# Two transformer blocks on one core: stacked query parts, state-space weights on ScalarE, 512-column token-major products

## The chip, the cores and the metric

The kernel runs on one core of a Trainium2 chip. The metric is the device time of one execution in microseconds (us). The engines are TensorE (PE; its weight loads are listed apart as PEld), VectorE (DVE), ScalarE (ACT), GpSimd (POOL) and SyncE (SP), which issues the transfers.

## The reference

Two blocks act one after the other on 512 tokens of 1024 features, in 32-bit floating point. What the change touches lies nearly all in the first:

```python
proj = h @ w_in                       # q, k, v, z, xbc, dt, two gates
attn = windowed_gqa_sink(q, k, v, attn_sink)      # 16 heads of 64, 4 key heads
ssd = ssd_branch(z, xbc, dt_raw, ...)             # 32 heads of 64 in 8 groups
merged = sigmoid(gate_a) * (attn @ w_attn_branch) + sigmoid(gate_b) * (ssd @ w_ssd_branch)
x = x + merged @ w_out
x = x + cross_attention(rmsnorm(x), rmsnorm(mem), w_xq, w_xkv, w_xo)
x = x + square(relu(rmsnorm(x) @ w_up)) @ w_down
```

In the attention a block of 128 queries sees 384 keys (256 at the ends), with a linear bias by distance and a sink. The state-space part works on chunks of 128 tokens, forward and backward, with step sizes `dt` of their own. Inside a chunk, token `l` takes from token `s` the product of C and B, times the decay `exp(cs[l] - cs[s])`, times the step of `s`: the forward direction for `l >= s`, the backward one for `l <= s`, both on the diagonal. Chunk states carry the rest, and a skip `d_skip * x` is added. The second block (gated delta rule, sparse attention, a mixture of experts) ends its mixing with `x + merged @ w_out_2`.

## The kernel before

Every dense product is made in split form: an operand is held as a rounded high part and the remainder, and `mm3` (L275) issues three matmuls, high by high (L277), high by low (L278) and low by high (L279). Weights come in units of 512 KB; `load_w` (L261) takes one into the buffer `wr`, ScalarE casts the high part `wh` (L269), VectorE, or for some units GpSimd, subtracts to get the low part `wl` (L272). There are two buffers each of `wh` and `wl`, so the cast of a unit waits until TensorE is done with the unit two before it.

`proj_b` (L281) makes feature-major products: 128 weight columns stand in the array and 512 tokens stream. `proj_a` (L303) and `add_units` (L866) make token-major ones: a tile of 128 tokens stands in the array and 256 weight columns stream; VectorE adds each result to the residual rows (L876). These are `w_out`, `w_xo`, `w_down` and, in the second block, `w_out2`.

In `attention`, the queries of two heads are one unit, `atH` high and `atL` low, one head in partitions 0 to 63 and the other in 64 to 127; the scores `sc` of a block of 128 queries are three matmuls with 64 rows. VectorE adds the bias and takes the maximum (L508).

The state-space part runs over eight groups of four heads. `ssd_in` projects and convolves (first tap on ScalarE, L631; the others on VectorE, L638). `ssd_p1` works chunk by chunk: GpSimd makes `xw` (L710) and the step matrix `D` (two masked multiplications L696, a sum L698), TensorE the chunk's states `st` (L717), evicted by ScalarE to `pv` (L721, L723). Rows of `cs` are read back from DRAM, spread over the partitions. Per head ScalarE subtracts the column value (L731) and VectorE subtracts that of the other direction and takes the smaller (L732). Then come the exponential on ScalarE (L734), two multiplications on VectorE (by `CB`, L735; by `D`, L736), the skip `sk` on GpSimd (L738), and the product `yd` (L741) of four 64-column matmuls. `ssd_p2` carries the states on (L759), makes `yo`, adds it head by head (L772), and multiplies by the gate; `ssd_p3` norms, transposes and splits into `yh`, `yl`.

A scheduler sets each engine's order when the program is built: it interleaves the inner part of a group with the dense products of others (`mm`), and an engine then works strictly in that order. A block of the program below is thus not a stretch of time.

Of the kernel before, what the change touches and what calls it, by code (L numbers as in the profile page):

```python
# [14 lines left out]
OP = mybir.AluOpType  # L15
# [23 lines left out]
def host_arrays(inp):  # L39
# [30 lines left out]
    out["w_out"] = units_a(f("w_out")[0])  # L70
# [3 lines left out]
    out["w_xo"] = units_a(f("w_xo")[0])  # L74
    out["w_up"] = units_bt(f("w_up")[0])
    out["w_down"] = units_a(f("w_down")[0])
# [26 lines left out]
    out["w_out2"] = units_a(f("w_out_2")[0])  # L103
# [42 lines left out]
    c[1] = i[:, None] <= i[None, :]  # L146
    c[2] = i[:, None] >= i[None, :]
# [20 lines left out]
class Emit:  # L168
# [30 lines left out]
    def psum(self, stack, n, mm, sa, sm):  # L199
        """the eight banks: dense products, two kinds of chains"""  # L200
# [30 lines left out]
    # ---------------------------------------------------------------- tools  # L231
# [71 lines left out]
    def proj_a(self, banks, units, act):  # L303
        """token-major: banks: psum tiles, two token tiles of 256 columns each; act(k, t) -> (hi, lo)"""
# [11 lines left out]
    def split(self, hi, lo, src, scale=None):  # L316
        """hi + lo = src * scale (scale: per-partition AP or None)"""
# [11 lines left out]
    def rstd(self, out, ss, n, eps=EPS):  # L329
        """out = (ss / n + eps) ** -0.5"""  # L330
# [5 lines left out]
    def rsqrt(self, v, eps, scale=1.0, tile=None):  # L336
        """(scale * v + eps) ** -0.5: a first guess from the bits, then Newton's iteration"""
# [13 lines left out]
    def norm_out(self):  # L351
        """where normed rows go, transposed and split: put(t, h, x) takes half a tile; hT(k) -> (hi, lo)"""
# [14 lines left out]
    def norm_T(self, gname):  # L367
        """rmsnorm of token-major tiles, transposed and split: step(t, x) takes a tile"""
# [16 lines left out]
    def consts(self):  # L385
# [3 lines left out]
        self.ident, self.MU, self.ML = c[:, 0:128], c[:, 128:256], c[:, 256:384]  # L389
# [59 lines left out]
    def attn_in(self):  # L449
        nc, a = self.nc, self.a  # L450
        # keys: natural and half-swapped, split
        kn = self.A("kn", (128, 2, 2, 512), F32)
        for m in range(2):
            ps = self.PM()
            self.proj_b(ps, [self.w0 if m == 0 else self.wb(8 + m)], self.hB, True)
            nc.scalar.copy(kn[:, 0, m, :], ps)
            nc.sync.dma_start(kn[0:64, 1, m, :], kn[64:128, 0, m, :])
            nc.sync.dma_start(kn[64:128, 1, m, :], kn[0:64, 0, m, :])
        self.kh = self.A("kh", (128, 2, 2, 512))
        self.kl = self.A("kl", (128, 2, 2, 512))  # L460
        for s in range(2):
            for m in range(2):
                self.split(self.kh[:, s, m, :], self.kl[:, s, m, :], kn[:, s, m, :])
# [7 lines left out]
    def attention(self):  # L471
        nc, a = self.nc, self.a
        # the result of a tile of queries takes the place of the queries
        self.atH = [self.A("atH") for _ in range(2)]
        self.atL = [self.A("atL") for _ in range(2)]
        for i in range(8):
            ps = self.PM()
            self.proj_b(ps, [self.wb(i)], self.hB)
            qh, ql = self.atH[i // 4][:, i % 4, :], self.atL[i // 4][:, i % 4, :]
            nc.scalar.activation(qh, ps, AF.Copy, scale=0.125)  # L480
            nc.vector.scalar_tensor_tensor(ql, ps, 0.125, qh.bitcast(F32), op0=OP.mult, op1=OP.subtract)
        for i in range(8):
            qh, ql = self.atH[i // 4][:, i % 4, :], self.atL[i // 4][:, i % 4, :]
# [4 lines left out]
            for hf in range(2):  # L488
# [3 lines left out]
                pr = slice(64 * hf, 64 * hf + 64)  # L492
                sw = 0 if hf == n % 2 else 1
                kh, kl = self.kh[pr, sw, n // 2, :], self.kl[pr, sw, n // 2, :]
# [5 lines left out]
                for b in range(4):  # L500
# [5 lines left out]
                    self.mm3(sc[:, :L], qh[pr, qs], ql[pr, qs], kh[:, k0:k1], kl[:, k0:k1], True, True)  # L506
# [44 lines left out]
    def dt_section(self):  # L551
# [45 lines left out]
        self.ncs = self.cp.tile([128, 4, 32], F32, name="ncs")  # L597
        nc.vector.tensor_scalar(self.ncs, self.cs[:, :, 0, :], -1.0, None, op0=OP.mult)
# [3 lines left out]
    def gates1(self, f0, f1):  # L602
        """tanh of the halved gates, feature-major, to DRAM"""
# [10 lines left out]
    def branch_a(self):  # L614
        """(1 + tanh(ga / 2)) * (attn @ Wa), feature-major, to DRAM"""
# [11 lines left out]
    def conv(self, ps, ct, ntap, first, silu_scale=True):  # L627
        """half of the centred depthwise convolution of a psum tile, then 2 * half * sigmoid = silu"""
# [15 lines left out]
    def ssd_in(self, g):  # L644
        """projections of group g: B, C, x (feature-major, convolved) and the doubled silu of z (token-major)"""
# [18 lines left out]
    def ssd_p1(self, g, inp):  # L664
        """the part inside the chunks, and the chunks' states"""
# [4 lines left out]
        # token-major x and B  # L670
# [20 lines left out]
        D = []  # L691

        def steps(c):
            d = [self.G("D", (128, 4, 128)) for _ in range(2)]
            for i, m in enumerate((self.MU, self.ML)):
                nc.gpsimd.tensor_tensor(d[i], m[:, None, :].to_broadcast([128, 4, 128]),  # L696
# [169 lines left out]
    def add_units(self, xs, src, nk, act, scale=1.0, last=True, then=None):  # L866
# [11 lines left out]
        if not last:  # L878
            return
# [1432 lines left out]
```

## Time and profile before

| | |
|---|---|
| median of 3 runs | 2178.56 us (2176.49, 2178.56, 2189.05) |
| profiled execution | span 2182.1 us; the page gives no other time for it |
| PE | 2033.9 us busy, 93% of the span, 11818 matmuls; mean granted clock 0.961 of full speed |
| DVE | 1362.7 us, 62% |
| ACT | 892.3 us, 41% |
| POOL | 504.9 us, 23% |
| moved | 266.71 MB, mean 122 GB/s |

The shares are averages over stages that differ. By the lines that run in them, attention lies at about 80 to 280 us of the span, the state-space part at 280 to 882, cross attention at 882 to 1040 with the output product of the mixing ahead of it, the feed-forward part at 1040 to 1360, and the second block behind it. A line of the trace gives the start, the busy time of the instruction (neighbours overlap, so the distance of two starts tells what one costs in a run of them), engine, line, operation, the names of output and inputs, the shape, and in brackets the idle time of the engine before it and what ended it.

### The profile page before, as it was taken

The page shows a single profiled execution, that of the slowest core. Times are in us where ns is not written, and L with a number is a line of the kernel's source. Part 1 is how long each engine was busy: PE and PEld are TensorE (multiplying, and loading weights), DVE is VectorE, ACT ScalarE, POOL GpSimd, SP SyncE. Part 2 cuts the span into 40 slices and gives each one's busy share as a digit, 9 for nine tenths or more (in the row PEclk, how much of TensorE's full clock was granted, in tenths as well). Part 3 has the DMA queues.
Part 4 walks back from the last instruction along what each step waited for, and adds up shares of the span by engine and source line. Part 5 has one row for each costly group of instructions (what it writes and reads, how often), then busy time and mean ns, then how long its engine had stood idle before and what let it go on. Part 6 is the DMA issues. An engine that isn't in the chain of part 4 may idle for free. (4 is left out here: it accounts for less than half of the span.)

```text
span 2182.1 us, 31237 instructions
## 1 busy us (share of the span) xinstructions
PE 2033.9 (93%) x11818; PEld 1730.2 (79%) x11818; DVE 1362.7 (62%) x2622; ACT 892.3 (41%) x1630; POOL 504.9 (23%) x515
## 2 busy tenths in 40 slices
PE   7999988989999988999999999899899999998995
PEld 7788877877787777888999999787878768886774
DVE  4566446786978765466334444667789452538885
ACT  4344434444545343254323222542232333246773
POOL 0000034034433142101111101503511110224444
PEclk9999999999999999999999999998899899998997
DMA  4211234323333254422222223224212104677976
GB/s 168 84 67 63 78 101 159 116 72 112 94 107 100 88 157 157 156 88 69 97 97 96 88 97 116 97 79 122 91 50 76 45 21 158 223 296 245 324 269 165
DMA packets 131302, 266.71 MB, mean 122 GB/s; under 512 B 22256, under 2 KB 67696, under 8 KB 127050
## 3 DMA queue, kind: packets, MB, share of 16 engines
q1 hardware_dynamic: 127690, 256.26, 35.5%
q0 software_dynamic: 3456, 8.39, 1.7%
q8 instruction: 95, 1.56, 0.3%
q14 instruction: 61, 0.50, 0.1%
HBM read 242.93 MB, written 25.35 MB: 123 GB/s over the span
## 5 line engine op out<-in xcount | busy, mean ns | idle before, releaser
L272 DVE TENSOR_TENSOR wl<-wr,wh 128x1024 fp32r<-128x1024 f32 (+1 forms) x272 | 316.4, 1164 | 288.9 <-ACT wh L269 277.9
L269 ACT CAST wh<-wr 128x1024 fp32r<-128x1024 f32 (+1 forms) x272 | 264.5, 973 | 548.5 <-PE mm L278 282.8
L279 PE MATMUL mm<-hTh,wl 128*128 128x512 f32 (+1 forms) x1056 | 412.4, 391 | 1.3 <-DVE wl L272 1.3
L277 PE MATMUL mm<-hTh,wh 128*128 128x512 f32 (+1 forms) x1056 | 411.9, 390 | 1.6 <-ACT hTh L320 0.9
L278 PE MATMUL mm<-hTl,wh 128*128 128x512 f32 (+1 forms) x1056 | 410.7, 389 | 0.8 <-DVE hTl L321 0.8
L279 PEld LDWEIGHTS mm<-hTh,wl 128*128 128x128 f32 x1056 | 203.4, 193 | 42.4 <-issue 5.1
L277 PEld LDWEIGHTS mm<-hTh,wh 128*128 128x128 f32 x1056 | 203.2, 193 | 39.6 <-issue 2.6
L278 PEld LDWEIGHTS mm<-hTl,wh 128*128 128x128 f32 x1056 | 203.2, 192 | 39.2 <-issue 3.2
L710 POOL TENSOR_TENSOR xw<-xt,dtT 128x256 f32<-128x256 f32 (+1 forms) x32 | 29.8, 932 | 551.4 <-ACT xt L678 551.4
L278 PE MATMUL mm<-wl,hTh 128*128 128x256 f32 x512 | 150.1, 293 | 0.0
L277 PE MATMUL mm<-wh,hTh 128*128 128x256 f32 x512 | 149.8, 293 | 0.0
L279 PE MATMUL mm<-wh,hTl 128*128 128x256 f32 x512 | 149.3, 292 | 0.0
L278 PE MATMUL mm<-wl,uh 128*128 128x256 f32 x512 | 145.0, 283 | 0.0
L279 PE MATMUL mm<-wh,ul 128*128 128x256 f32 x512 | 144.8, 283 | 0.0
L277 PE MATMUL mm<-wh,uh 128*128 128x256 f32 x512 | 144.7, 283 | 0.0
L876 DVE SCALAR_TENSOR_TENSOR x<-mm,x 128x256 f32<-128x256 f32 x152 | 57.5, 420 | 93.4 <-PE mm L279 92.8
L1042 POOL TENSOR_TENSOR ul<-r,uh 128x512 fp32r<-128x512 f32 x32 | 41.7, 1303 | 274.8 <-ACT uh L1041 274.8
L278 PEld LDWEIGHTS mm<-wl,hTh 128*128 128x128 f32 x512 | 100.9, 197 | 1.7 <-issue 0.7
L277 PEld LDWEIGHTS mm<-wh,hTh 128*128 128x128 f32 x512 | 100.8, 197 | 1.0 <-issue 0.2
L279 PEld LDWEIGHTS mm<-wh,hTl 128*128 128x128 f32 x512 | 100.8, 197 | 0.7 <-issue 0.5
L278 PEld LDWEIGHTS mm<-wl,uh 128*128 128x128 f32 x512 | 98.2, 192 | 0.5 <-DVE wl L272 0.2
L277 PEld LDWEIGHTS mm<-wh,uh 128*128 128x128 f32 x512 | 98.2, 192 | 0.3
(571 smaller groups left out, 4706.2 us busy)
## 6 DMA issues: line engine op xcount, KB each, us to landing
mr<-in_w_egu_dram SPq DMA_DIRECT2D x32, 1024.0 KB, 8.4
wr<-in_win_b_dram SPq DMA_DIRECT2D x59, 512.0 KB, 3.3
cs<-csd SPq DMA_DIRECT2D x64, 256.0 KB, 4.5
wr<-in_w_up_dram SPq DMA_DIRECT2D x32, 512.0 KB, 3.3
wr<-in_w_down_dram SPq DMA_DIRECT2D x32, 512.0 KB, 3.3
wr<-in_w_ed_dram SPq DMA_DIRECT2D x32, 512.0 KB, 4.5
wr<-in_w_b_dram SPq DMA_DIRECT2D x29, 512.0 KB, 3.3
wr<-in_win_a_dram SPq DMA_DIRECT2D x18, 512.0 KB, 3.3
```

What stands on the lines that cost most here:

```text
L269: nc.scalar.copy(w.hi, raw)
L272: e.tensor_tensor(w.lo, raw, w.hi.bitcast(F32), op=OP.subtract)
L277: mm(out, lh, rh, start=start, stop=False, skip_group_check=skip)
L278: mm(out, lh, rl, start=False, stop=False, skip_group_check=skip)
L279: mm(out, ll, rh, start=False, stop=stop, skip_group_check=skip)
L710: nc.gpsimd.tensor_tensor(xw[:, d0:d1], h3(xt[c])[:, None].to_broadcast([128, d1 - d0, 4, 64]), self.dtdec[:, c, d0:d1, H][:, :, :, None]. ...
L876: nc.vector.scalar_tensor_tensor(xv, ps[t // 2][:, (t % 2) * 256:(t % 2 + 1) * 256], scale, xv, op0=OP.mult, op1=OP.add)
L1042: nc.gpsimd.tensor_tensor(ul[:, j, :], r, uh[:, j, :].bitcast(F32), op=OP.subtract)
```

## The change

Attention: keys are kept so that each key head stands in both halves of the partitions. For an even head `atH` holds the high part of its queries in partitions 0 to 63 and the low part in 64 to 127; `atL` does so for the odd head with the halves swapped. The scores are then two matmuls of 128 rows: both query parts by the high keys, and both by the low keys.

State space: `D` comes from ScalarE, one activation per head of a sign matrix with half the difference of the two steps as scale and half their sum as bias; `twice` doubles the diagonal of `CB`. ScalarE also subtracts the column values of both directions, and makes `sk` head by head. VectorE multiplies `D` by `CB`, takes the minimum and multiplies by `D`, 512 columns at once. The states' part takes 512 or 256 columns at once.

Token-major products: `w_down`, `w_xo` and the first half of the columns of `w_out` and `w_out2` go 512 columns wide, in four banks; the last block of `w_xo` and of `w_down` keeps its units on chip and goes token tile by token tile.

```diff
 def attn_in(self):
+        h0, h1 = slice(0, 64), slice(64, 128)
...
-            nc.scalar.copy(kn[:, 0, m, :], ps)
-            nc.sync.dma_start(kn[0:64, 1, m, :], kn[64:128, 0, m, :])
-            nc.sync.dma_start(kn[64:128, 1, m, :], kn[0:64, 0, m, :])
+            for e, (own, other) in enumerate(((h0, h1), (h1, h0))):
+                nc.scalar.copy(kn[own, m, e, :], ps[own])
+                nc.sync.dma_start(kn[other, m, e, :], kn[own, m, e, :])
...
 def attention(self):
-            qh, ql = self.atH[i // 4][:, i % 4, :], self.atL[i // 4][:, i % 4, :]
-            nc.scalar.activation(qh, ps, AF.Copy, scale=0.125)
-            nc.vector.scalar_tensor_tensor(ql, ps, 0.125, qh.bitcast(F32), op0=OP.mult, op1=OP.subtract)
+            for q, own, other in ((self.atH, slice(0, 64), slice(64, 128)), (self.atL, slice(64, 128), slice(0, 64))):
+                q = q[i // 4][:, i % 4, :]
+                nc.scalar.activation(q[own], ps[own], AF.Copy, scale=0.125)
+                nc.vector.scalar_tensor_tensor(q[other], ps[own], 0.125, q[own].bitcast(F32), op0=OP.mult, op1=OP.subtract)
...
-                    self.mm3(sc[:, :L], qh[pr, qs], ql[pr, qs], kh[:, k0:k1], kl[:, k0:k1], True, True)
+                    nc.tensor.matmul(sc[:, :L], q[:, qs], kh[:, k0:k1], start=True, stop=False)
+                    nc.tensor.matmul(sc[:, :L], q[:, qs], kl[:, k0:k1], start=False, stop=True)
...
 def ssd_p1(self, g, inp):
-        nc.scalar.copy(CB, ps.rearrange("p (c l) -> p c l", c=4))
-            for i, m in enumerate((self.MU, self.ML)):
-                nc.gpsimd.tensor_tensor(d[i], m[:, None, :].to_broadcast([128, 4, 128]),
-                                        self.dt[:, c, i, H][:, :, None].to_broadcast([128, 4, 128]), op=OP.mult)
-            nc.gpsimd.tensor_tensor(d[0], d[0], d[1], op=OP.add)
+        nc.vector.tensor_tensor(CB, ps.rearrange("p (c l) -> p c l", c=4), self.twice[:, None, :].to_broadcast([128, 4, 128]), op=OP.mult)
...
             for h in range(4):
-                nc.scalar.activation(cb[0][:, h, :], cb[0][:, h, :], AF.Identity, bias=self.ncs[:, c, 4 * g + h:4 * g + h + 1])
-                nc.vector.scalar_tensor_tensor(cb[0][:, h, :], cb[1][:, h, :], self.cs[:, c, 1, 4 * g + h:4 * g + h + 1],
-                                               cb[0][:, h, :], op0=OP.subtract, op1=OP.min)
+                hh = slice(4 * g + h, 4 * g + h + 1)
+                for d in range(2):
+                    nc.scalar.activation(cb[d][:, h, :], cb[d][:, h, :], AF.Identity, bias=self.ncs[:, c, d, hh])
+                nc.scalar.activation(D[:, h, :], self.sgn, AF.Identity, bias=self.hs[:, 0, c, hh], scale=self.hs[:, 1, c, hh])
+            nc.vector.tensor_tensor(D, D, CB[:, c, None, :].to_broadcast([128, 4, 128]), op=OP.mult)
+            nc.vector.tensor_tensor(cb[0], cb[0], cb[1], op=OP.min)
             nc.scalar.activation(cb[0], cb[0], AF.Exp)
-            nc.vector.tensor_tensor(cb[0], cb[0], CB[:, c, None, :].to_broadcast([128, 4, 128]), op=OP.mult)
-            nc.vector.tensor_tensor(cb[0], cb[0], D[c], op=OP.mult)
+            nc.vector.tensor_tensor(cb[0], cb[0], D, op=OP.mult)
-            nc.gpsimd.tensor_tensor(sk, h3(xt[c]), self.dskip[:, H][:, :, None].to_broadcast([128, 4, 64]), op=OP.mult)
+            for h in range(4):
+                nc.scalar.activation(sk[:, h, :], xt[c][:, 64 * h:64 * h + 64], AF.Copy, scale=self.dskip[:, 4 * g + h:4 * g + h + 1])
...
 def ssd_p2(self, g, st, yh, yl, j0):
-                for h in range(4):
-                    hs = slice(64 * h, 64 * h + 64)
-                    nc.vector.scalar_tensor_tensor(pv[c][:, d, hs], pv[p][:, d, hs], self.tot[:, p, d, 4 * g + h:4 * g + h + 1],
-                                                   pv[c][:, d, hs], op0=OP.mult, op1=OP.add)
+        for k in range(2):
+            q = self.G("pq", (128, 2, 256))
+            nc.vector.tensor_tensor(v(q), v(pv[k]), self.stp[:, k, :, H][:, :, :, None].to_broadcast([128, 2, 4, 64]), op=OP.mult)
+            nc.vector.tensor_tensor(pv[k + 1], pv[k + 1], q, op=OP.add)
...
-                for h in range(4):
-                    hs = slice(64 * h, 64 * h + 64)
-                    nc.vector.scalar_tensor_tensor(y[:, hs], po[:, 256 * d + 64 * h:256 * d + 64 * h + 64],
-                                                   self.ecs[:, c, d, 4 * g + h:4 * g + h + 1], y[:, hs],
-                                                   op0=OP.mult, op1=OP.add)
+            nc.vector.tensor_tensor(v(yo)[:, d0:d1], v(po.rearrange("p (d e) -> p d e", d=2))[:, d0:d1],
+                                    self.ecs[:, c, d0:d1, H][:, :, :, None].to_broadcast([128, d1 - d0, 4, 64]), op=OP.mult)
+            for d in range(d0, d1):
+                nc.vector.tensor_tensor(y, y, yo[:, d], op=OP.add)
...
+    def wide(self, srcs, act, done, resident=False):
+        n = len(srcs)
+        if resident:
+            U = [self.load_w(w, 2, 512) for w in srcs]
+            step = yield
+        ps = [None] * 4
+
+        def part(u, i, t):
+            for j in range(2):
+                ah, al = act(2 * i + j, t)
+                self.mm3(ps[t], ah, al, u.hi[:, j, :], u.lo[:, j, :], i + j == 0, i == n - 1 and j == 1)
+            if i == n - 1:
+                done(t, ps[t])
...
+            ps[:] = [self.PA(), self.PA(), self.PA(), self.PS()]
+            for i in range(n):
+                u = self.load_w(srcs[i], 2, 512)
+                for t in range(4):
+                    part(u, i, t)
...
 def ffn(self, xs):
-            self.add_units(xs, a["w_down"][:, c:c + 1], 1, act, last=c == 7, then=self.last_norm if c == 7 else None)
+            self.add_units(xs, [self.units("w_down", n, 2 * c, 2) for n in range(2)], None, act, last=c == 7,
+                           then=self.last_norm if c == 7 else None)
```

On TensorE, in the attention, a run of scores between two products of other units; before (`ot` is the transposition of the result of the unit before, L277 to L279 are the three parts of `mm3`):

```order
L540 MATMUL ot<-consts,o 128x128 x4
L277 MATMUL sc<-kh,atH 128x256
L278 MATMUL sc<-kl,atH 128x256
L279 MATMUL sc<-kh,atL 128x256
L277 MATMUL sc<-kh,atH 128x384
L278 MATMUL sc<-kl,atH 128x384
L279 MATMUL sc<-kh,atL 128x384
```

and after (L509 and L510 are the two matmuls of a score, L279 to L281 the three of `mm3`):

```order
L544 MATMUL ot<-consts,o 128x128 x4
L509 MATMUL sc<-kh,atH 128x256
L510 MATMUL sc<-kl,atH 128x256
L509 MATMUL sc<-kh,atH 128x384
L510 MATMUL sc<-kl,atH 128x384
```

The third matmul of each score is gone; the number of runs of scores between other products is 40 before and 51 after.

On ScalarE, in the state-space part, the stretch around one chunk of the fourth group; before (`wh` are the casts of weights, `cs` the decays, `cv` and `ct` the convolution, `pv` the states):

```order
L269 CAST wh<-wr 128x1024
L721 COPY pv<-st 128x256
L723 COPY pv<-st 128x256
L731 ACTIVATE cs<-cs,ncs 128x128 x4
L640 ACTIVATE ct<-cv 128x512
L631 ACTIVATE cv<-mm,vecs 128x512
L734 ACTIVATE cs<-cs 128x512
L269 CAST wh<-wr 128x512
```

and after:

```order
L271 CAST wh<-wr 128x1024
L726 COPY pv<-st 128x256
L740 ACTIVATE D<-consts,hs 128x128 x4
L738 ACTIVATE cs<-cs,ncs 128x128 x8
L747 ACTIVATE sk<-xt,vecs 128x64 x4
L654 ACTIVATE ct<-cv 128x512
L743 ACTIVATE cs<-cs 128x512
L645 ACTIVATE cv<-mm,vecs 128x512
L271 CAST wh<-wr 128x1024
```

Between two casts of weights there stood 4 small activations and an exponential of one chunk, and now stand 16 small ones and an exponential.

## Rows read from the trace of the kernel before

**Rows 1.** Windows by stage: length, busy us of each engine (instructions), clock, DMA, GB/s.

```profile
80.00:280.00 200.00, 199.99 (x1202) 167.75 (x1201) 115.16 (x267) 87.90 (x216) 0.00 (x0) 1.00 0.21 69
280.00:882.00 602.00, 547.94 (x2829) 458.10 (x2828) 442.18 (x891) 267.59 (x566) 203.80 (x188) 0.95 0.38 119
...
1040.00:1360.00 320.00, 320.00 (x2052) 292.92 (x2051) 135.01 (x217) 95.21 (x120) 44.09 (x34) 1.00 0.30 98
```

**Rows 2.** Waits of PE, 280 to 882 us: total, times, longest.

```profile
PE yd L741 <- DVE cs L736: 42.2, 17, 5.7
```

**Rows 3.** Timeline of PE: the longest stall, its idle time in brackets.

```profile
316.56 1.94 PE L741 MATMUL yd<-xt,cs 128*128 128x64 f32 x8 [5.66 <-DVE cs L736]
```

**Rows 4.** Windows of 5 us behind that stall.

```profile
315.00:320.00 5.00, 3.44 (x12) 3.19 (x13) 1.83 (x2) 0.04 (x1) 3.88 (x5) 0.50 0.56 182
320.00:325.00 5.00, 5.00 (x16) 3.96 (x16) 2.89 (x8) 3.31 (x8) 2.45 (x3) 0.67 0.23 68
```

**Rows 5.** Timeline of PE: first and last of even runs, 256 and 512 columns.

```profile
1069.75 0.28 PE L279 MATMUL mm<-wh,ul 128*128 128x256 f32 x1
...
1081.27 0.28 PE L279 MATMUL mm<-wh,ul 128*128 128x256 f32 x1
...
1099.76 0.39 PE L278 MATMUL mm<-hTl,wh 128*128 128x512 f32 x1
...
1102.94 0.39 PE L277 MATMUL mm<-hTh,wh 128*128 128x512 f32 x1
```

**Rows 6.** Instructions of L277: durations min/median/max, first and last start, forms.

```profile
L277 PE MATMUL mm<-wh,uh x512: 278/283/283, 1066.3 to 1383.3; 128*128 128x256 f32 x171
...
L277 PE MATMUL mm<-wh,mh x256: 278/283/386, 882.2 to 1954.3; 128*128 128x256 f32 x128
...
L277 PE MATMUL mm<-wh,oh x64: 278/283/385, 980.3 to 1018.2; 128*128 128x256 f32 x64
```

**Rows 7.** Timeline of PE around a run of scores.

```profile
150.44 0.28 PE L277 MATMUL mm<-wh,hTh 128*128 128x256 f32 x1
150.65 0.44 PE L277 MATMUL sc<-kh,atH 64*128 64x384 f32 x1
...
151.95 0.28 PE L279 MATMUL mm<-wh,hTl 128*128 128x256 f32 x1
```

**Rows 8.** Lines by form, 280 to 882 us: busy, mean ns, idle before, releasers.

```profile
L696 POOL TENSOR_TENSOR D<-consts,dtT 128x512 f32<-128x512 f32 x64 | 77.6, 1233 | 1.1 <-PE yd L741 1.1
...
L732 DVE SCALAR_TENSOR_TENSOR cs<-cs,dtT 128x128 f32<-128x128 f32 x128 | 53.4, 475 | 16.5 <-DMA cs<-csd 10.4 <-ACT wh L269 4.3 <-ACT cs L731 1.5
```

**Rows 9.** Instructions of L732: who waited for it (us, times).

```profile
  ACT cs L734: 42.6, 17
```

**Rows 10.** Timeline of VectorE: L732 in two places.

```profile
587.05 3.16 DVE L732 SCALAR_TENSOR_TENSOR cs<-cs,dtT 128x128 f32<-128x128 f32 x4
...
598.59 1.13 DVE L732 SCALAR_TENSOR_TENSOR cs<-cs,dtT 128x128 f32<-128x128 f32 x4
```

**Rows 11.** Timeline of ScalarE in the state-space part.

```profile
573.72 0.91 ACT L789 ACTIVATE y<-y,rsy 128x256 f32<-128x256 f32 x2 [0.84 <-POOL rsy L334]
574.53 0.62 ACT L734 ACTIVATE cs<-cs 128x512 f32<-128x512 f32 x1
...
581.59 0.37 ACT L721 COPY pv<-st 128x256 f32<-128x256 f32 x1 [0.82 <-PE st L717]
581.86 0.38 ACT L723 COPY pv<-st 128x256 f32<-128x256 f32 x1
...
582.80 1.28 ACT L731 ACTIVATE cs<-cs,ncs 128x128 f32<-128x128 f32 x4
...
590.96 0.63 ACT L640 ACTIVATE ct<-cv 128x512 f32<-128x512 f32 x1
591.50 0.76 ACT L631 ACTIVATE cv<-mm,vecs 128x512 f32<-128x512 f32 x1
592.16 1.03 ACT L269 CAST wh<-wr 128x1024 fp32r<-128x1024 f32 x1
```

More of the change, by code (lines that the diff above doesn't have):

```diff
@@ L69, in host_arrays @@
     out["w_sb"] = units_bt(f("w_ssd_branch")[0], 4)
-    out["w_out"] = units_a(f("w_out")[0])
+    out["w_out_w"] = units_a(f("w_out")[0][:, :512], 512, 2)
+    out["w_out"] = units_a(f("w_out")[0][:, 512:])
     out["w_xq"] = units_bt(f("w_xq")[0])
@@ L73, in host_arrays @@
     out["w_xv"] = units_a(f("w_xkv")[0][:, 512:])
-    out["w_xo"] = units_a(f("w_xo")[0])
+    out["w_xo"] = units_a(f("w_xo")[0], 512, 2)
     out["w_up"] = units_bt(f("w_up")[0])
-    out["w_down"] = units_a(f("w_down")[0])
+    out["w_down"] = units_a(f("w_down")[0], 512, 2)
     for n in ("norm_mix", "norm_cross", "norm_mem", "norm_ffn"):
@@ L864, in branch_b @@
                 self.split(self.mh[f // 4][:, f % 4, :], self.ml[f // 4][:, f % 4, :], ma)
-    def add_units(self, xs, src, nk, act, scale=1.0, last=True, then=None):
+    def wide(self, srcs, act, done, resident=False):
[10 more added lines that the diff above has]
+                done(t, ps[t])
+        if resident:
+            for t in range(4):
+                ps[t] = self.PM()
+                for i in range(n):
+                    part(U[i], i, t)
+                if step:
+                    step(t)
+        else:
+            ps[:] = [self.PA(), self.PA(), self.PA(), self.PS()]
+            for i in range(n):
+                u = self.load_w(srcs[i], 2, 512)
+                for t in range(4):
+                    part(u, i, t)
+        yield
@@ L869, in add_units, with add @@
+    def add_units(self, xs, wide, src, act, scale=1.0, last=True, then=None):
         nc = self.nc
-        n = 4 - 2 // nk if last else 4
+        def add(t, ps, c0, w):
+            xv = xs[t][:, c0:c0 + w]
+            nc.vector.scalar_tensor_tensor(xv, ps, scale, xv, op0=OP.mult, op1=OP.add)
+        n = len(wide)
         for i in range(n):
+            done = lambda t, ps: add(t, ps, 512 * i, 512)
+            if last and src is None and i == n - 1:
+                go = self.wide(wide[i], act, done, True)
+                next(go)
+                step = then() if then else None
+                go.send((lambda t: step(t, xs[t])) if step else None)
+            else:
+                for _ in self.wide(wide[i], act, done):
+                    pass
+        if src is None:
+            return
+        nb = src.shape[0]
+        for i in range(nb - 1):
@@ L872, in add_units @@
             ps = [self.PM() for _ in range(2)]
-            self.proj_a(ps, [self.load_w(src[i, h], 4, 256) for h in range(nk)], act)
+            self.proj_a(ps, [self.load_w(src[i, h], 4, 256) for h in range(2)], act)
             for t in range(4):
-                xv = xs[t][:, i * 256:(i + 1) * 256]
-                nc.vector.scalar_tensor_tensor(xv, ps[t // 2][:, (t % 2) * 256:(t % 2 + 1) * 256], scale, xv,
-                                               op0=OP.mult, op1=OP.add)
-        if not last:
-            return
@@ L894, in add_units, with units @@
             if step:
                 step(t, xs[t])
+    def units(self, name, n, i0, cnt):
+        return [self.a[name][n, i0 + i] for i in range(cnt)]
     def w_out(self, name, act, scale):
         xs = self.load_x()
-        self.add_units(xs, self.a[name], 2, act, scale, then=self.then("norm_cross"))
+        self.add_units(xs, [self.units(name + "_w", 0, 0, 4)], self.a[name], act, scale, then=self.then("norm_cross"))
         self.dump_x("x1", xs)
@@ L1025, in cross @@
         act = lambda k, t: (oh[:, k, t * 128:(t + 1) * 128], ol[:, k, t * 128:(t + 1) * 128])
-        self.add_units(xs, a["w_xo"], 1, act, then=self.then("norm_ffn"))
+        self.add_units(xs, [self.units("w_xo", n, 0, 2) for n in range(2)], None, act, then=self.then("norm_ffn"))
         self.dump_x("x2", xs)
```

74 lines of the change are left out of this document (35 added, 39 removed).

## The prediction

> **What bounds the kernel now.** I read the busy shares stage by stage first. In the attention (80 to 280 us) and in the feed-forward part (1040 to 1360 us) TensorE is busy for all of the 200 and 320 us: there every matmul that goes, or gets shorter, comes off the end [rows 1]. In the state-space stage (280 to 882 us) TensorE idles 54 of 602 us, and its mean clock is 0.95 of full speed, another 30 us (0.05 of 602) [rows 1]. The view of waits names the idle time: in 17 places TensorE's state-space product `yd` waits for VectorE's last multiplication, 42.2 us in all [rows 2]. The timeline shows the worst, 5.66 us [rows 3]. The clock by 5 us windows shows what follows: 0.50, then 0.67 [rows 4]. With 3.44 us of work in the first of these, the loss is 0.50 x 3.44 + 0.33 x 5 = 3.4 us behind one stall. So a stall costs itself and often about as much again in clock. In this stage VectorE has 442 us of work, GpSimd 204, ScalarE 268: none is full on average, and what counts is the order in which the chain behind one `yd` is worked off.
>
> **The change, part by part.**
>
> *Wide products.* Token-major products of 256 columns become half as many of 512. A 256-column matmul takes 0.120 us (96 intervals in 11.52 us), a 512-column one 0.227 us (14 in 3.18 us) [rows 5]: 2 x 0.120 - 0.227 = 0.013 us saved per pair. The rows count 512 instructions per line for `w_down`, 256 for the two output products (of which half become wide) and 64 for `w_xo`, on three lines each [rows 6]: 3 x (256 + 64 + 32) = 1056 pairs, **-13.6 us**. TensorE is full or nearly so where they stand. The four banks of one block are evicted tile by tile: 18 matmuls (4.1 us) lie between a tile's eviction and the need for its bank, so evictions stay hidden. Bounds: nothing, if the gap per instruction goes to something else, to 13.6.
>
> *Attention.* 64 score matmuls go (two of 128 rows do what three of 64 rows did): 32 of 256 and 32 of 384 columns. At 0.120 and, halfway between the rows of 256 and 512, 0.174 us: 3.84 + 5.57 = 9.4 us. The timeline also shows that the excursion into 64-row matmuls costs more than its streaming: from the matmul ahead of it to the second one behind it 1.51 us pass, where one and one of 256 columns outside and three and three inside (0.12 x 5 + 0.174 x 3) would take 1.12 [rows 7]. That leaves 0.39, half on entry and half on leaving. Of 40 such runs 17 stand between full 128-row split products on both sides, 21 on one side alone: 17 x 0.39 + 21 x 0.195 = 10.7 us. With 128 rows on both sides I expect it to go: **-20 us** in all; bounds 9.4 (if the extra comes from the switch of operand, not of rows) to 20. The price: each unit of queries is split by four half-height instructions in place of two, 8 more on ScalarE and 8 on VectorE at about 0.6 to 0.7 us, 5 us each. They lie beside TensorE's 200 full us, in which ScalarE works 88 and VectorE 115: nothing.
>
> *State-space stage.* GpSimd loses 128 instructions (`D`, `sk`), VectorE the four subtract-min per chunk (53.4 us) [rows 8]; in their place ScalarE gets per chunk four `D` activations, four more bias activations and four `sk` copies, and VectorE three wide multiplications in place of two, plus the wide forms in the states' part. VectorE also runs slowly while GpSimd works: the same four instructions took 3.16 us in one place and 1.13 in another [rows 10], and ScalarE's exponential waited 42.6 us for them [rows 9]. So the chain behind `yd` gets shorter on VectorE and longer on ScalarE.
>
> ScalarE's prices, by starts of neighbours: one 256-column eviction 0.27, two activations with a pointer on 256 columns 0.81, so 0.41 each; on 128 columns four in 1.28 us, of which the last counts with its whole length, as the eviction's 0.38, so 0.30 each [rows 11]. The slope is then 0.11 per 128 columns. The convolution's first tap (512 columns, two pointers) takes 0.66, so `D` (two pointers, 128 columns) would take 0.66 - 3 x 0.11 = 0.33; bounds 0.30 and 0.66. `sk` (64 columns) 0.245, at most 0.41. Per group: 16 x 0.33 + 32 x 0.30 + 16 x 0.245 + 4 exponentials at 0.54, like the tanh of the same size, = 20.9 us. In the order of the changed program the stretch from the first `st` to the fourth `yd` of a middle group also holds on ScalarE two `y`, two first taps, two tanh, three casts of about 1.0, six evictions and two `yh` of 512 columns like a tap: 9.1 us. Sum 30.0; with 0.5 for the first `st` and 0.8 for the last multiplication 31.3. TensorE has in that stretch of the fourth group 79 matmuls of 512 columns (17.9), 13 of 256 (1.6), and some 6.2 of `st`, `yd` and transposes at their own durations: 25.7. So it waits about 5 us there. Two groups are of this kind; four have 25 to 35 more matmuls there (29 us of work) and wait 2 to 3; the first two have 120 and more and wait for nothing. That is 20; casts and multiplications that stand in order behind other waits add 1 to 3 per group, 8 to 24. I take 36 for the 42.2 of now: **-6 us**, and leave the clock's loss as it is. Bounds are the rivals below.
>
> Sum: -13.6 - 20 - 6 = -39.6. The profiled execution has a span of 2182.1 us (the page gives no other time for it), 3.5 above the median of 2178.56. 2182.1 - 39.6 - 3.5 = **2139 us**. Block 2 but for its output product keeps its order: nothing.
>
> **Rivals.**
>
> *A, VectorE freed.* ScalarE is early enough, because its work needs only loaded rows and runs ahead while TensorE streams, and the 42.2 us of stalls fall to 10, VectorE no longer being slowed by GpSimd (77.6 us of `D` alone [rows 8]) nor late for the exponential. Then 32 us of idle time and about as large a share of the 30 us of clock go (32 / 42 x 30 = 22): 2139 + 6 - 32 - 22 = **2091**. For it: the slow VectorE and the wait for it [rows 9, 10]. Against: ScalarE's own sum. The Trainium skill, page "SBUF — State Buffer", section "Who interferes with whom", has VectorE instructions with two inputs in SBUF contend with GpSimd's reads, as the 3.16 against 1.13 us of the trace agrees. Chance 0.27.
>
> *B, ScalarE becomes the bound: slower.* Place: the 20.9 us per group ahead of the exponentials, with weight casts queued behind them. If `D` costs 0.66 and `sk` 0.41, the group gets 16 x 0.33 + 16 x 0.165 = 7.9 us more, on eight groups 64: 2139 + 64 = **2203**. It decides once ScalarE's sum per stretch passes about 34.5 us, where the extra stalls (4.5 on eight groups) eat the 39.6 of gains; that is 0.37 us for each of the 64 small activations in place of 0.30. Against it: the cost follows the columns [rows 11]. The Trainium skill, page "ScalarE: Activation LUTs", section "Rules for kernel authors", speaks against the change, since it puts additions and multiplications on VectorE; this trace shows them at 0.30 on ScalarE and 0.28 on VectorE (1.13 us for four). Chance 0.09.
>
> *C, the saving per matmul does not come*: wide pairs take as long as the two they replace, and the 0.39 remains. 2178.6 - 9.4 - 6 = **2163**. Against it: twelve microseconds of even spacing [rows 5]. The Trainium skill, page "TensorE: Matmul & The Clock Gate", section "Back-to-back issue gap", gives N / 2.4 + 2.5 ns for one matmul, by which a pair would save 2.5 ns; the rows have 13 ns. Chance 0.12.
>
> **How the numbers follow.** Forecast 0.52 (own range 2125 to 2157, stalls of 28 to 44 and attention of 9.4 to 20), A 0.27 (2075 to 2110), B 0.09, C 0.12. The range 2090 to 2180 leaves out half of A and most of B. About 1%, 22 us, is what a measurement can tell: faster is below 2157. Forecast and A but for their upper tails, and little of C, give 0.73; same (C, the better end of B, tails) 0.21; slower, the rest of B, 0.06.
>
> **What would show it.** The profile after should have feed-forward rows of 512 columns at 0.227 us and that stage some 10 us shorter (768 x 0.013); the attention stage some 20 shorter, without a 0.39 us matmul behind the scores; `D` rows at 0.33 and `sk` at 0.25 on ScalarE; and `yd` waiting about 36 us, with ScalarE's activations behind it. A is right if `yd`'s stalls fall to 10 and the stage's clock nears 1.00; B, if ScalarE is busy without a gap ahead of each `yd`; C, if the two full stages keep their length. The forecast is wrong if weight casts, queued on ScalarE behind state-space work, become what TensorE's dense products wait for.

## The result, and the profile after

The changed kernel takes 2152.7 us (median of 4 runs, 2143.17 to 2159.65) against 2182.16 of the kernel before, 2178.56 in the runs shown ahead; the ratio is 0.986, 95% interval 0.9826 to 0.9894. That is 30 us less, where 40 had been forecast. The profiled execution has a span of 2150.0 us, 32 less than before.

The state-space part up to the last product of `yh`, and the feed-forward part from the first to the last product of `uh`, in windows of both traces: length, busy us of PE, PEld, DVE, ACT and POOL (instructions), clock, DMA, GB/s. Of the kernel before:

```profile
300.00:881.60 581.60, 527.55 (x2706) 441.61 (x2705) 434.88 (x872) 258.25 (x544) 203.39 (x188) 0.95 0.39 120
1066.30:1383.30 317.00, 315.93 (x2119) 292.96 (x2118) 138.62 (x231) 93.21 (x120) 45.61 (x40) 1.00 0.29 95
```

and of the changed one:

```profile
300.00:867.60 567.60, 512.41 (x2667) 430.39 (x2665) 364.30 (x572) 360.42 (x908) 46.68 (x56) 0.95 0.39 118
...
1053.30:1359.60 306.30, 305.25 (x1351) 252.24 (x1349) 131.70 (x169) 92.42 (x119) 44.72 (x39) 1.00 0.32 98
```

The feed-forward part is 10.7 us shorter and as full as before [rows 1]. In the state-space part VectorE has 71 us less work, GpSimd 157 less, ScalarE 102 more, and yet TensorE's idle time is 55 us (it was 54) and the clock 0.95. Counted from its own first state-space product `st` (at 301.4 us before, 296.9 after) to the last `yh`, the stage goes from 580.2 to 570.7 us. It is shorter only because more dense products were done ahead of it, beside the attention: 1916 matmuls of `mm` stand in it, where 1963 stood, 9.8 us less of their work.

The view of waits of TensorE in that stage of the changed kernel (total us, times, longest), which answers to [rows 2]:

```profile
PE yd L750 <- DVE cs L744: 23.8, 17, 3.2
PE mm L279 <- DVE cv L652: 9.3, 2, 4.7
PE mm L280 <- DVE wl L274: 8.5, 8, 1.2
PE mm L281 <- DVE wl L274: 5.8, 9, 1.0
PE mm L279 <- ACT wh L271: 3.0, 7, 1.0
```

The wait of `yd` has nearly halved; 26.6 us of waits of dense products (`mm`), of which 4.6 were there before, stand in its place. They wait for weights (`wh`, `wl`) and for a bank that the convolution frees (`cv`). The timeline around the second row's first wait shows who was late. ScalarE from 425 us on:

```profile
425.57 1.64 ACT L740 ACTIVATE D<-consts,hs 128x128 f32<-128x128 f32 x4
427.12 2.44 ACT L738 ACTIVATE cs<-cs,ncs 128x128 f32<-128x128 f32 x8
429.46 1.05 ACT L747 ACTIVATE sk<-xt,vecs 128x64 f32<-128x64 f32 x4
...
437.70 0.76 ACT L645 ACTIVATE cv<-mm,vecs 128x512 f32<-128x512 f32 x1
438.36 1.03 ACT L271 CAST wh<-wr 128x1024 fp32r<-128x1024 f32 x1
```

Its window, and the product of TensorE that waited, idle time in brackets:

```profile
425.00:447.00 22.00, 17.39 (x87) 14.67 (x85) 15.10 (x24) 21.77 (x61) 0.00 (x0) 0.85 0.34 92
```

```profile
443.79 0.55 PE L279 MATMUL mm<-wh,hTh 128*128 128x256 f32 x1 [4.62 <-DVE cv L652]
```

ScalarE is busy for 21.77 of 22 us. Behind two chunks of small activations it comes to the convolution's first tap at 437.70; VectorE's four taps follow, and the bank is free at 443.8. The releaser named is VectorE; the one that was late is ScalarE. The lines by form in the state-space part say the same of the chain behind `yd` (busy us, mean ns, idle time before and its releaser). They answer to [rows 8, 9, 11]:

```profile
L738 ACT ACTIVATE cs<-cs,ncs 128x128 f32<-128x128 f32 x256 | 81.3, 393 | 15.5 <-DMA cs<-csd 15.4
...
L740 ACT ACTIVATE D<-consts,hs 128x128 f32<-128x128 f32 x128 | 54.5, 487 | 0.0
L747 ACT ACTIVATE sk<-xt,vecs 128x64 f32<-128x64 f32 x128 | 35.3, 337 | 0.0
...
L742 DVE TENSOR_TENSOR cs<-cs 128x512 f32<-128x512 f32 x32 | 22.1, 691 | 50.0 <-ACT cs L738 48.8 <-issue 1.1
```

Before, ScalarE waited 42.6 us for VectorE's four instructions; now VectorE waits 48.8 us for ScalarE's.

### The profile page after: what moved, and what is told of

Same layout as the page of the kernel before. It is cut to its first block, busy times and chain, and to the rows that moved or that the text cites. A ratio compares the mean times of both kernels' runs of the same rounds, so it can differ in the third digit from the quotient of the medians.

```text
span 2150.0 us, 28810 instructions
## 1 busy us (share of the span) xinstructions
PE 1995.7 (93%) x10730; PEld 1662.3 (77%) x10730; DVE 1296.6 (60%) x2269; ACT 1007.3 (47%) x2016; POOL 352.3 (16%) x387
## 5 line engine op out<-in xcount | busy, mean ns | idle before, releaser
L274 DVE TENSOR_TENSOR wl<-wr,wh 128x1024 fp32r<-128x1024 f32 (+1 forms) x272 | 309.6, 1139 | 336.8 <-ACT wh L271 330.7
L281 PE MATMUL mm<-hTh,wl 128*128 128x512 f32 (+1 forms) x1056 | 410.6, 389 | 3.4 <-DVE wl L274 3.4
L279 PE MATMUL mm<-hTh,wh 128*128 128x512 f32 (+1 forms) x1056 | 410.5, 389 | 3.2 <-ACT wh L271 2.1
L281 PEld LDWEIGHTS mm<-hTh,wl 128*128 128x128 f32 x1056 | 203.1, 192 | 43.3 <-DVE wl L274 6.1
L279 PEld LDWEIGHTS mm<-hTh,wh 128*128 128x128 f32 x1056 | 203.2, 193 | 39.8 <-ACT wh L271 3.6
L279 PE MATMUL mm<-wh,hTh 128*128 128x256 f32 x512 | 152.2, 299 | 9.7 <-DVE cv L652 9.3
L281 PE MATMUL mm<-wh,hTl 128*128 128x256 f32 x512 | 150.4, 295 | 0.0
L279 PEld LDWEIGHTS mm<-wh,hTh 128*128 128x128 f32 x512 | 103.0, 202 | 11.9 <-ACT cs L738 10.0
L280 PEld LDWEIGHTS mm<-wl,hTh 128*128 128x128 f32 x512 | 102.9, 201 | 10.7 <-DVE wl L274 10.6
L281 PEld LDWEIGHTS mm<-wh,hTl 128*128 128x128 f32 x512 | 102.8, 201 | 0.1
L652 DVE SCALAR_TENSOR_TENSOR cv<-mm,vecs,cv 128x510 f32<-128x510 f32 (+1 forms) x128 | 95.3, 745 | 10.6 <-ACT cv L645 9.7
L738 ACT ACTIVATE cs<-cs,ncs 128x128 f32<-128x128 f32 x256 | 81.3, 393 | 15.5 <-DMA cs<-csd 15.4
L279 PE MATMUL sa<-wh,uh 128*128 128x512 f32 x180 | 70.0, 389 | 0.0
L280 PE MATMUL sa<-wl,uh 128*128 128x512 f32 x180 | 70.0, 389 | 0.0
L281 PE MATMUL sa<-wh,ul 128*128 128x512 f32 x180 | 70.0, 389 | 0.0
L750 PE MATMUL yd<-xt,cs 128*128 128x64 f32 x256 | 38.1, 297 | 23.8 <-DVE cs L744 23.8
```

The costliest lines, as they stand in the source:

```text
L274: e.tensor_tensor(w.lo, raw, w.hi.bitcast(F32), op=OP.subtract)
L279: mm(out, lh, rh, start=start, stop=False, skip_group_check=skip)
L280: mm(out, lh, rl, start=False, stop=False, skip_group_check=skip)
L281: mm(out, ll, rh, start=False, stop=stop, skip_group_check=skip)
L652: nc.vector.scalar_tensor_tensor(ov, iv, self.cw(ct, tap), ov, op0=OP.mult, op1=OP.add)
L738: nc.scalar.activation(cb[d][:, h, :], cb[d][:, h, :], AF.Identity, bias=self.ncs[:, c, d, hh])
```

## The experiments

All ratios are to the kernel before, with 95% intervals. "First block" is the time of the last product of `uh` in the trace: 1383.3 us before, 1359.6 after. "The stage" is the state-space stage from its first `st` to the last product of `yh`: 580.2 us before, 570.7 after. Each kernel has one trace.

**Each part alone.** The edits are the diff's hunks of one part, on the kernel before.

```diff
 # attn_only: attn_in, attention
-                    self.mm3(sc[:, :L], qh[pr, qs], ql[pr, qs], kh[:, k0:k1], kl[:, k0:k1], True, True)
+                    nc.tensor.matmul(sc[:, :L], q[:, qs], kh[:, k0:k1], start=True, stop=False)
+                    nc.tensor.matmul(sc[:, :L], q[:, qs], kl[:, k0:k1], start=False, stop=True)
```

> The kernel before with the stacked query parts alone. Theory (streaming and entry into 64-row matmuls both go): about 19 us less than before, with the scores at their own streaming times and no longer gap on entering or leaving them. Rival (only the 64 matmuls go, the gaps stay): about 9 us less. Rival (the splits on ScalarE and VectorE come on the path): no change.

Measured: 2160.45 us, ratio 0.9899 (0.9845 to 0.9953), -22 us; first block 1361.1, also -22. The full size of the first theory. A run of scores between dense products, in the changed kernel's timeline of TensorE:

```profile
131.31 0.40 PE L281 MATMUL mm<-hTh,wl 128*128 128x512 f32 x1
131.55 0.33 PE L509 MATMUL sc<-kh,atH 128*128 128x384 f32 x1
131.72 0.34 PE L510 MATMUL sc<-kl,atH 128*128 128x384 f32 x1
131.90 0.28 PE L509 MATMUL sc<-kh,atH 128*128 128x256 f32 x1
132.01 0.28 PE L510 MATMUL sc<-kl,atH 128*128 128x256 f32 x1
132.13 0.40 PE L279 MATMUL mm<-hTh,wh 128*128 128x512 f32 x1
132.37 0.40 PE L280 MATMUL mm<-hTl,wh 128*128 128x512 f32 x1
```

From 131.31 to 132.37 pass 1.06 us, where streaming alone is 2 x 0.227 + 2 x 0.174 + 2 x 0.12 = 1.04: of the 0.39 us of [rows 7] 0.02 is left at this place. At others some remains: the run that starts at 153.56 us has 0.28 for its first score of 384 columns, where 0.174 was expected.

```diff
 # ssd_only: consts, dt_section, ssd_p1, ssd_p2
-                nc.vector.scalar_tensor_tensor(cb[0][:, h, :], cb[1][:, h, :], ...)
+                nc.scalar.activation(D[:, h, :], self.sgn, AF.Identity, bias=..., scale=...)
```

> The kernel before with the new state-space part alone. Theory (ScalarE, with some 21 us of small activations per group, now makes weight casts and first convolution taps late, and the idle time moves from the product yd to the dense products): no change within 5 us; yd waits about 24 us in place of 42, dense products wait about 20 us more than before, mean clock of the stage still 0.95. Forecast on record: 6 us less. Rival (VectorE freed from GpSimd's slowing): 30 to 50 us less, clock near 1.00.

Measured: 2180.01 us, ratio 0.9973 (0.9944 to 1.0003); first block 1389.3, 6 us longer than before. In its trace `yd` waits 27.3 us and dense products 23.8 (42.2 and 4.6 before), and the stage takes 584.8 us, 4.6 longer. The runs can't tell it from no change, and the forecast's -6 lies in their interval. The trace of the stage speaks against -6: in traces with the same state-space part the stage repeats within 2.1 us (580.2 and 582.3 with `wide_only`; 566.6 and 566.5 with `attn_only` and `no_ssd`).

```diff
 # wide_only: host arrays, add_units, w_out, cross, ffn
-            self.add_units(xs, a["w_down"][:, c:c + 1], 1, act, ...)
+            self.add_units(xs, [self.units("w_down", n, 2 * c, 2) for n in range(2)], None, act, ...)
```

> The kernel before with the 512-column products alone. Theory (0.013 us for each of 1056 pairs, all on TensorE's path): 13 to 14 us less, of which 10 in the feed-forward part. Rival (the isolated gap of 2.5 ns per matmul is all that is saved): 3 us less. Rival (the first columns of the output products, with four banks for one block, wait for evictions): the feed-forward part gives its 10 us and the output products nothing, 10 us less.

Measured: 2164.55 us, ratio 0.9902 (0.987 to 0.9934), -21 us with 14 in the interval. In the trace the feed-forward part takes 306.4 us, 10.6 less, and from the last `yh` product to the end of `w_xo` it is 136.7 us as it was (136.6): nothing from the output products of the first block. The first block as a whole is 7.5 us shorter (1375.8); the rest of the -21 lies in the second block, which is 12 us shorter in this trace; below on what that is worth. In the changed kernel 512-column products start 0.227 us apart (16 intervals in 3.63 us), in the feed-forward part as elsewhere [rows 5]:

```profile
1059.82 0.39 PE L281 MATMUL sa<-wh,ul 128*128 128x512 f32 x1
...
1063.45 0.39 PE L279 MATMUL sm<-wh,uh 128*128 128x512 f32 x1
```

**All but the state-space part.** The two edits above together.

```diff
 # no_ssd: attn_only and wide_only
-            D = self.G("D", (128, 4, 128))
+            steps(c)
```

> The changed kernel with the state-space part as before. Theory (the new state-space part is worth nothing): as long as the changed kernel, 2150 us, within 5 us. Forecast on record: 6 us longer than the changed kernel. Rival (it is worth more than it looks, and the other parts less): 15 us or more longer than the changed kernel.

Measured: 2142.45 us, ratio 0.9808 (0.9767 to 0.9849), 10 us less than the changed kernel; first block 1348.6, 11 less. The intervals of the two ratios overlap. Of the 11 us, 6.4 lie ahead of the first `st` (290.5 us here, 296.9 in the changed kernel), where both do the same work, with 1706 and 1705 matmuls. The windows from 60 to 80 us show why, first here and then in the changed kernel:

```profile
60.00:80.00 20.00, 18.56 (x88) 14.30 (x87) 14.47 (x26) 8.45 (x13) 0.00 (x0) 1.00 0.33 90
60.00:80.00 20.00, 18.56 (x67) 14.17 (x66) 14.79 (x31) 6.74 (x10) 0.00 (x0) 0.74 0.29 86
```

TensorE idles 1.44 us in each, 1.2 of it in one wait, and only in the changed kernel's trace does the clock fall behind it, to 0.50 between 70 and 75 us. The trace of `sk_pool` below, with the changed state-space part but for `sk`, stays at 1.00 there, and that of `d_sk_pool` falls in the same way; so the fall is not that part's doing. Comparisons of first blocks with the changed kernel hold some 6 us of it. In the stage itself the difference is 4.2 us (570.7 against 566.5): with the other parts in, the new state-space part costs some 4 us, as it does alone.

**Work off ScalarE.** From here on the edits are on the changed kernel.

```diff
 # sk_pool
-            for h in range(4):
-                nc.scalar.activation(sk[:, h, :], xt[c][:, 64 * h:64 * h + 64], AF.Copy, scale=...)
+            nc.gpsimd.tensor_tensor(sk, h3(xt[c]), self.dskip[:, H][:, :, None].to_broadcast([128, 4, 64]), op=OP.mult)
```

> The changed kernel with the skip sk back on GpSimd (one instruction per chunk). Theory (ScalarE's queue is the local bound of the state-space part): 35 us off ScalarE, a fifth of its small activations; idle time of TensorE in the stage from 55 to about 45 us, the first block some 8 us shorter than in the changed kernel (about 2143). Rival (VectorE or the written order of the dense products holds it): no change. Rival (GpSimd slows VectorE): longer by up to 5 us.

Measured: 2126.68 us, ratio 0.976 (0.9704 to 0.9816), 26 us less than the changed kernel; first block 1329.3, 30 less, of which 7 lie ahead of the first `st` and are the changed kernel's fall of the clock. The stage is 23.3 us shorter (547.4), three times what I expected: each us taken off ScalarE, 30 in the stage, gave most of a us back. Idle time and clock go together there: TensorE idles 16.3 us less and needs 7 us less for the same number of matmuls.

```diff
 # d_sk_pool: sk_pool, and
-                nc.scalar.activation(D[:, h, :], self.sgn, AF.Identity, bias=self.hs[:, 0, c, hh], scale=self.hs[:, 1, c, hh])
+            nc.gpsimd.tensor_tensor(D, self.sgn[:, None, :].to_broadcast([128, 4, 128]), bc(1), op=OP.mult)
+            nc.gpsimd.tensor_tensor(D, D, bc(0), op=OP.add)
```

> The changed kernel with sk and the step matrix D back on GpSimd (D as two instructions of 512 columns); the bias of both directions stays on ScalarE, the wide minimum and multiplications on VectorE. Theory (ScalarE's queue): 90 us off ScalarE, idle time in the stage below 30 us and clock up with it, 20 to 30 us shorter than the changed kernel (about 2127). Rival (GpSimd's work slows VectorE's chain, as before the change): idle time 45 to 50 us, as long as the kernel without the new state-space part (2142).

Measured: 2107.61 us, ratio 0.9665 (0.9627 to 0.9702), 45 us less than the changed kernel; first block 1319.0, the stage 531.1, 39.6 less. The dense products' waits are gone but for 5.5 us; the window of the stage has 32 us idle and a clock of 0.98:

```profile
295.00:826.00 531.00, 499.30 (x2680) 424.05 (x2679) 386.98 (x573) 284.65 (x658) 161.98 (x155) 0.98 0.42 127
```

```diff
 # d_dve: sk_pool, and D by the same two instructions on VectorE
+            nc.vector.tensor_tensor(D, self.sgn[:, None, :].to_broadcast([128, 4, 128]), bc(1), op=OP.mult)
+            nc.vector.tensor_tensor(D, D, bc(0), op=OP.add)
```

> sk on GpSimd and D on VectorE as two instructions of 512 columns, 44 us more there, 54 less on ScalarE. Theory (it is ScalarE that must be relieved, whoever takes the work): shorter than with sk alone on GpSimd (2127), about 2117, though less than with D on GpSimd (2108). Rival (the gain of D on GpSimd came from GpSimd making it ahead of the chain; VectorE is as close to the bound as ScalarE): as long as with sk alone moved, or longer.

Measured: 2098.58 us, ratio 0.9636 (0.9597 to 0.9675), the shortest. So for `D` it was ScalarE that had to be relieved, whoever took the work. I had ranked GpSimd ahead of VectorE; the runs don't bear that out, nor the reverse, as the two intervals overlap. The stage's window:

```profile
290.00:815.00 525.00, 497.76 (x2683) 423.07 (x2683) 409.87 (x638) 284.92 (x659) 84.04 (x91) 0.99 0.43 129
```

VectorE carries 410 of 525 us and TensorE idles half as long as in the changed kernel: 27 us, of which `yd` 12.4.

```diff
 # d_sk_dve: d_dve, and
-            nc.gpsimd.tensor_tensor(sk, ...)
+            nc.vector.tensor_tensor(sk, ...)
```

> D and sk both on VectorE, nothing of the weights on GpSimd or ScalarE. sk adds 32 x 0.41 = 13 us to VectorE's 415 of 531 and takes GpSimd's 30 us away, while which VectorE's wide multiplications took up to 0.79 in place of 0.69. Theory (ScalarE was the bound, GpSimd's remaining work costs VectorE a little): 0 to 8 us less than with D alone on VectorE (2098). Rival (VectorE, at over 80%, is now the bound): 5 to 15 us longer.

Measured: 2100.27 us, ratio 0.9637 (0.9593 to 0.9682): no difference from the one before, neither theory's side. In the trace the stage is 5.6 us longer (530.2), at the rival's lower end.

**More work on ScalarE.**

```diff
 # sk_twice
+            for _ in range(2):
                 for h in range(4):
                     nc.scalar.activation(sk[:, h, :], xt[c][:, 64 * h:64 * h + 64], AF.Copy, scale=...)
```

> The changed kernel with the four sk activations of every chunk made twice (the second time the same values). Theory (ScalarE's queue is the local bound): some 31 us more on ScalarE; moving as much away was worth 26 us, so 15 to 25 us longer than the changed kernel (about 2172). Rival (moving sk only happened to give a better written order of the dense products): within 5 us of the changed kernel.

Measured: 2186.49 us, ratio 1.0034 (0.9999 to 1.0069), 34 us more than the changed kernel, and more than the 25 expected. The window of the stage and the wait of `yd`:

```profile
297.00:908.00 611.00, 519.93 (x2651) 434.38 (x2650) 364.93 (x570) 389.05 (x1034) 47.16 (x56) 0.91 0.37 108
```

```profile
PE yd L751 <- DVE cs L744: 63.7, 25, 6.6
```

TensorE has as many matmuls in the stage as in the changed kernel (2679 and 2680), and VectorE as much work; 29 us more of ScalarE gave 36 us more of idle time and a clock of 0.91 in place of 0.95. The stage, from its first `st`, is 617.5 us, 46.8 longer. With the removal of `sk` this is the same lever in both directions, and a lucky order of the dense products is no longer needed as an explanation.

**Where ScalarE's relief does not help.**

```diff
 # cast_pool: in load_w, while the state-space part runs
+        if self.inssd and self.wn % 2:
+            nc.gpsimd.tensor_copy(w.hi, raw)
+        else:
+            nc.scalar.copy(w.hi, raw)
```

> The changed kernel with the cast of every second weight unit on GpSimd while the state-space part runs. Theory (casts queued on ScalarE behind the small activations make the dense products late): the 17 us that dense products wait for weights fall by half or more and the stage gets 10 us shorter (about 2142). Rival (the dense products wait because TensorE's written order brings them too early, and any engine is late): waits for weights stay, with GpSimd named in place of ScalarE. Rival (GpSimd's cast is slow): the stage gets longer.

Measured: 2151.08 us, ratio 0.987 (0.9823 to 0.9917), no change. GpSimd's cast of 128x1024 takes 1.07 us, ScalarE's 1.04. TensorE's waits in the stage:

```profile
PE yd L754 <- DVE cs L748: 27.2, 17, 3.4
PE mm L283 <- ACT cs L747: 6.0, 1, 6.0
PE mm L283 <- ACT sk L751: 4.9, 1, 4.9
PE mm L285 <- DVE wl L278: 3.3, 5, 0.7
PE mm L284 <- DVE wl L278: 2.7, 3, 1.1
PE mm L283 <- ACT wh L276: 2.5, 5, 0.9
```

The waits for weights fell by half, from 17.3 to 8.5 us, as the theory wanted; 10.9 us of waits of dense products on ScalarE's `cs` and `sk` came instead, and `yd` waits 3.4 more. Late casts alone were not the lever: what stands behind the small activations is late, and here the cast is only one of the things that stand there. Nor is it ScalarE's total that counts: its work in the stage falls to 330 us, as with `sk` on GpSimd (332), and the time does not fall. VectorE has 18 us more work in this stage and GpSimd twice as much, 97 us; what they cost was not separated.

```diff
 # p2_only: no_ssd, and ssd_p2 as changed
+            nc.vector.tensor_tensor(v(q), v(pv[k]), self.stp[:, k, :, H][:, :, :, None].to_broadcast([128, 2, 4, 64]), op=OP.mult)
+            nc.vector.tensor_tensor(pv[k + 1], pv[k + 1], q, op=OP.add)
```

> Stacked queries, wide products, and of the state-space part only the wide VectorE operations for the carried states (the part inside the chunks as before). If VectorE is what made yd late before the change: its 25 us of saved work show, 5 to 15 us less than without the new state-space part (about 2132). If only the chain of exponential and GpSimd's slowing counts: no change (2142).

Measured: 2150.14 us, ratio 0.9887 (0.9852 to 0.9922), and not less than without it (2142.45): the wide operations for the states gain nothing by themselves. In the trace the stage is even 12 us longer (578.5 for 566.5), and VectorE has 12 us less work in it, not the 25 expected; the edit also makes 32 more matmuls, as the `yo` products of 512 columns become two of 256. `yd` waits 50.4 us there (41.9 without it); the four subtract-min of VectorE, with GpSimd beside them, take 536 ns each (475 before).

```diff
 # bias_pool: d_sk_pool, and
-                for d in range(2):
-                    nc.scalar.activation(cb[d][:, h, :], cb[d][:, h, :], AF.Identity, bias=self.ncs[:, c, d, hh])
+                nc.scalar.activation(cb[0][:, h, :], cb[0][:, h, :], AF.Identity, bias=self.ncs[:, c, 0, hh])
+            nc.gpsimd.tensor_tensor(cb[1], cb[1], self.ncs[:, c, 1, H][:, :, None].to_broadcast([128, 4, 128]), op=OP.add)
```

> sk and D on GpSimd and the bias of the second direction too, as one instruction of 512 columns per chunk: 38 us more off ScalarE, some 40 on GpSimd. Theory: ScalarE, at 289 of 539 us, still makes yd late; 5 to 10 us shorter than 2108. Rival (by now the waits are VectorE's last multiplication and the loads of cs, and GpSimd's instruction, over 1 us, stands in the chain and slows VectorE): no change or up to 10 us longer.

Measured: 2141.11 us, ratio 0.9826 (0.9788 to 0.9863), 33 us longer than with `sk` and `D` on GpSimd, far more than the rival's 10. The lines by form in its state-space part:

```profile
L738 POOL TENSOR_TENSOR cs<-cs,ncs 128x512 f32<-128x512 f32 x32 | 37.3, 1167 | 60.4 <-DMA cs<-csd 60.4
L742 DVE TENSOR_TENSOR D<-D,CB 128x512 f32<-128x512 f32 x32 | 36.5, 1141 | 14.8 <-POOL D L741 14.8
L743 DVE TENSOR_TENSOR cs<-cs 128x512 f32<-128x512 f32 x32 | 31.2, 975 | 12.8 <-POOL cs L738 12.8
```

GpSimd, in order, waits 60 us for the rows of `cs`, so what stands behind that instruction, `D` above all, is late; and VectorE's `D` by `CB` takes 1141 ns, where it took 966 with `sk` and `D` on GpSimd and 689 in the changed kernel. ScalarE is down to 249 us and it does not help. Which of the two costs more was not separated.

## Why the prediction was right or wrong

The sign, the range and the size (30 us less for 40 forecast) hold; two terms came out, and one had the wrong sign. By its own steps:

*Attention, -20*: right, -22 alone in both measures, with most of the gap gone where it was looked at.

*Wide products, -13.6*: right where most of it lay. 768 of the 1056 pairs give 10.6 us in place of 10.0, 0.014 each. The 192 pairs of the first block's other products (2.5 us by the forecast) show nothing; TensorE was not full there, 149 of 158 us of that stage, and "full or nearly so" was one step too far. The last 96 pairs stand in the second block, whose traces differ by more than they could save.

*State-space part, -6*: wrong. By the traces the stage became 4.6 us longer by it alone and 4.2 beside the other parts. That makes 10 us against the forecast's -6, as much as separates 30 from 40. The step that failed is "I take 36 for the 42.2 of now": it put all of ScalarE's lateness on `yd`. The wait of `yd` came out at 23.8, better than the 36, while 26.6 us fell on dense products, in the one wait followed up behind the same queue. The text named that case (weight casts queued on ScalarE) as what would make the forecast wrong, but gave it neither a term nor a chance. ScalarE's sum was nearly right: bias 0.29 and `sk` 0.24 as estimated (differences of the runs of four and eight above), `D` (1.64 - 0.49) / 3 = 0.38 in place of 0.33, 0.8 us per group. The Trainium skill, page "ScalarE: Activation LUTs", section "What ACT_TABLE_LOAD costs", gives 186 ns + 0.833 per column + 93 per pointer operand, less 93 of overlap; by an estimate from these figures `D` would cost 0.39. The trace agrees with its 0.38, better than my slope.

*Rival A* (VectorE freed, 2091) had the first half right: VectorE's work fell from 435 to 364 us and its multiplication by `CB` runs undisturbed at 0.69. It did not become time while VectorE waited for ScalarE. With `D` and `sk` off ScalarE much of it did: 2098.6.

*Rival B* (ScalarE bound, slower than before) was the mechanism at work, at part of its price: the 30 us of gains elsewhere stand against it. It put the point of no gain at a sum per stretch of 34.5 us. With 30.0 of the forecast, 0.8 for `D` and 31 / 8 = 3.9 for a second `sk` the sum is 34.7, and that kernel measured 1.0034 (0.9999 to 1.0069): the point was met. It is one point, and the gains elsewhere came to 30 to 35 us in place of 39.6, so part of that is luck.

*Rival C* is out: 512-column rows at 0.227, 256 at 0.120.

What stays open: a scheduler lays out the order anew for every edit, so part of each step's size may be its order; the dose of ScalarE's work in both directions shows the direction and that it is large, not that it is all. From more of ScalarE's work to less, the stage takes 617.5 us with 393 us of it (`sk` twice), 570.7 with 363 (changed), 547.4 with 332 (`sk` moved) and 524.6 with 285 (`D` and `sk` moved); but 575.3 with 330 where casts were moved, and 565.0 with 249 where GpSimd took a bias into the chain.

## What to carry to other kernels

An engine at 64% of a stage can be its bound if it works in order and the chain that others wait for passes through it in bursts: sum its work between two hand-offs, not over the stage, and ask what else stands in its queue. When a change moves a wait, add up all idle time of the waiting engine, not that of the line it used to wait at. Four short instructions per chunk on the engine of the chain cost more than two long ones on an engine that is fuller on average: VectorE at 78% of the stage was the better place for `D` than ScalarE. Measure a stage from its own first instruction to its own last, as what happened ahead of it shifts every later time.

## What the runs showed of the hardware

The second block takes 783 to 802 us in the traces of kernels that share its code (802 with `sk` on GpSimd, 793 with `D` there too, 783 with `sk` twice), at mean granted clocks of 0.93, 0.94 and 0.96. That is as much as the spread of runs of one kernel (2143 to 2160), and it is why a stage by its trace tells differences of 10 us that four runs of the whole don't.

As much idle time can cost clock or not: behind 1.44 us of idle time between 60 and 70 us the granted clock stayed at 1.00 in the trace of `no_ssd` and fell to 0.50, the lower of its two levels, in that of the changed kernel. The part ahead of the state-space stage took 6.4 us longer there, 5.7 of it TensorE's busy time for the same matmuls.

VectorE's multiplication of `D` by `CB` (128x512, both inputs on chip) is slower the more GpSimd works in the stage: 689 ns with 47 us of GpSimd's work (changed kernel), 791 with 84 (`D` on VectorE), 966 with 162 (`D` and `sk` on GpSimd), 1141 with 207 (`bias_pool`).
